# Decoder layer on one core: the merge and output stages with a recorded load queue, five gate buffers, w_o's second half split later, and another last norm

## Chip, cores, metric

One core of a Trainium2 chip runs the whole program in one launch. The metric is the device time of one execution in microseconds. Engines are named as in the profile: PE is TensorE, PEld its weight loads, DVE is VectorE, ACT is ScalarE, POOL is GpSimd, SP is SyncE, which here only issues transfers.

## What is computed

One decoder layer over 1024 tokens of width 1024, batch 1, all in float32. Only the end of it is touched here:

```
merged = sigmoid(g_conv) * y_conv + sigmoid(g_att) * y_att     # y_att = (att * silu(z_att)) @ w_att_out
x = x + gate * (merged @ w_o)
out = rmsnorm(x) * final_g                                     # x * rsqrt(mean(x*x) + 1e-6) * final_g
```

What comes before it (norm, in-projection, convolution branch, dilated window attention in three groups) is left as it is.

## The kernel before, in words

Products in float32 are made of three products of rounded parts: each operand is split into a high part `hi` (rounded to the type float32r by a copy on ACT, line 57) and a low part `lo` (the difference, on DVE, line 58; the helper is `split`, lines 55 to 58). `mm3` (lines 72 to 75) issues hi·hi, hi·lo and lo·hi into one bank of PSUM.

The merge (lines 1197 to 1224) makes eight tiles `d` of 128 output channels by 1024 tokens, kept transposed (channels in partitions). For tile d, `project` runs two halves of 512 tokens; each half has four steps k, twelve matmuls, over the attention output `ah`, `al` with the weights `w_ao[d]` (256 KB), which were loaded to a buffer `wraw` and split into `whi` and `wlo`. The function `merge` (lines 1219 to 1222) takes the bank: DVE multiplies it by the sigmoid of the attention gate (`sgr`, 512 KB, loaded from the scratch tensor `ascr`; sigmoid on ACT, line 1205), DVE adds the convolution part (`ttr`, 512 KB, from `cscr`), and the sum is split into `hh[d]` and `hl[d]`, the left operand of the output product. The 16 `ascr` half tiles were written by the stage before, through small buffers `gs` (lines 791, 792), the last of them just as the merge begins.

`w_o` has two halves n (512 output columns each) of four parts kp of 512 KB. `w_out` loads and splits one part into `woh[n, kp]`, `wol[n, kp]`. The parts (0,0) to (0,2) are done in the attention stage, (0,3), (1,0) and (1,1) inside the merge at d = 1, 3, 5 (lines 1214 to 1216), and (1,2), (1,3) are recorded behind it (lines 1227 to 1229).

The output (lines 1236 to 1278) makes eight tiles `t` of 128 tokens by 1024 columns. `out_cols` runs 24 matmuls per 512 columns over `hh`, `hl` and w_o, then DVE multiplies by the gate row `gate_b`, adds the residual `xt`, and ACT squares the result and sums it over the columns. `out_norm` makes the inverse root of the mean by a square root on ACT, a reciprocal and one Newton step on DVE (`inv_sqrt`, lines 106 to 114), scales `y` by it and by `final_g` in two halves (line 1266) and writes each half (line 1267). The order is (0,0), (1,0), (0,1), (1,1) by tile and column half, then tiles 2 to 7 whole; tile 7's second half is cut in two pieces of 256 columns, so that it has three sums.

Buffers: `wraw` has three buffers, `whi` and `wlo` two each. The pool `fin` of the last two stages lies over memory of the attention stage's pool, buffer by buffer (a tile waits only for those old tiles that it lies over). Its ring `tmp` holds `sgr`, `ttr`, `xt` and `y` in four buffers of 4 KB per partition.

What sets the order: the attention stage runs in the recorded order on PE, DVE, ACT and SP (`manual_schedule`, line 1133). Behind it, in the merge and the output, a planner sets the order of each engine's instructions and of SP's queue by priorities and its own model of times; each queue is in order at run time, so a waiting instruction holds all that stand behind it.

Of the kernel before, what the change touches and what calls it, by code (L numbers as in the profile page):

```python
# [39 lines left out]
def layer(ctx: ExitStack, tc: tile.TileContext, a, out):  # L40
    nc = tc.nc
    ctx.enter_context(nc.allow_non_contiguous_dma(reason="small gathers of row maxima"))
    add, mult, sub, mx = ALU.add, ALU.mult, ALU.subtract, ALU.max
# [3 lines left out]
    wpool = ctx.enter_context(tc.tile_pool(name="wpool", bufs=2))  # L47
# [48 lines left out]
    gscr = dram.tile([1, D], F32, name="gscr")  # L96
    bscr = dram.tile([2, 512], F32, name="bscr")
    cscr = dram.tile([KT, P, S], F32, name="cscr")
    ascr = dram.tile([KT, P, S], F32, name="ascr")
# [6 lines left out]
    def inv_sqrt(cols, n, tmp):  # L106

        s, y, z = tmp[:, 0:n], tmp[:, n:2 * n], tmp[:, 2 * n:3 * n]
        nc.scalar.activation(s, cols, AF.Sqrt)
        nc.vector.reciprocal(y, s)  # L110
        nc.vector.tensor_mul(z, y, y)
        nc.vector.tensor_mul(z, z, cols)
        nc.vector.tensor_scalar(z, z, -0.5, 1.5, op0=mult, op1=add)
        nc.vector.tensor_mul(cols, y, z)

# [3 lines left out]
    def bank():  # L119
        return pd.tile([P, 512], F32, name="d", tag="d")  # L120
# [50 lines left out]
    with sbuf_pool("start") as st, tc.manual_schedule(  # L171
            engines={nc.tensor.engine, nc.vector.engine, nc.scalar.engine, nc.sync.engine}):
# [192 lines left out]
        for t in range(7):  # L365
# [4 lines left out]
            if t == 3:  # L370
                last = bank()
# [10 lines left out]
        for kt in range(KT):  # L382
# [424 lines left out]
    raws, made_w = {}, {}  # L807
# [34 lines left out]
    k2, q2, v2 = {}, {}, {}  # L842
# [227 lines left out]
    ATT = (("k0", "k1"), ("k2", "q0"), ("q1", "q2"), ("l0", "l1"))  # L1070
    woh, wol = {}, {}

    def w_out(n, kp, pool=None):


        raw = load_raw(a["w_o"][n, kp])
        if not pool and (n, kp) < (0, 3):
            yield
        if pool:
            hi, lo = (pool.tile([P, 1024], F32R, name=f"{x}{n}{kp}") for x in ("oh", "ol"))  # L1080
        elif n == 0 and kp > 1:
            both = parts_tile("oh")
            hi, lo = both[:, 0], both[:, 1]
        else:
            hi, lo = (head_tile(x, "oh") for x in {(0, 0): ("l2", "v0"), (0, 1): ("v1", "v2"), (1, 3): ("k0", "k1")}[n, kp])
        (split if pool or (n, kp) >= (0, 3) else split_late)(hi, lo, raw)
        woh[n, kp], wol[n, kp] = hi, lo
        yield

# [43 lines left out]
    with tc.manual_schedule(engines={nc.tensor.engine, nc.vector.engine, nc.scalar.engine, nc.sync.engine}):  # L1133
        for slot_ in range(-LEAD, 4 * units - LEAD):
# [6 lines left out]
            if VAL <= slot_ < stages + VAL:  # L1141
                n, st_ = divmod(slot_ - VAL, 8)
# [4 lines left out]
            if TURN <= slot_ < stages + TURN:  # L1147
                n, st_ = divmod(slot_ - TURN, 8)
# [3 lines left out]
            if 0 <= slot_ < stages:  # L1152
                n, st_ = divmod(slot_, 8)
# [39 lines left out]
    ahead = ahead_ao[0]  # L1193
# [3 lines left out]
    pd = ctx.enter_context(psum_pool("pd3", bufs=8))  # L1197
    fp = ctx.enter_context(sbuf_pool("fin"))
    def temp4(name):
        return fp.tile([P, S], F32, name=name, tag="tmp", bufs=4)  # L1200

    def gates_load(d):
        sg_, tt = temp4("sgr"), temp4("ttr")
        nc.sync.dma_start(sg_, ascr[d])
        nc.scalar.activation(sg_, sg_, AF.Sigmoid)
        nc.sync.dma_start(tt, cscr[d])
        return sg_, tt

    ahead = ahead, gates_load(0)
    for d in range(KT):  # L1210
        w, (sg_, tt) = ahead
        if d + 1 < KT:
            ahead = weights(a["w_ao"][d + 1], 512), gates_load(d + 1)
        if d in (1, 3, 5):
            for _ in w_out(*((0, 3), (1, 0), (1, 1))[d // 2], fp if d > 1 else None):
                pass
        hi, lo = hh[:, d, :], hl[:, d, :]

        def merge(half, s, ps):
            nc.vector.tensor_mul(sg_[:, s], ps, sg_[:, s])  # L1220
            nc.vector.tensor_add(tt[:, s], tt[:, s], sg_[:, s])
            split(hi[:, s], lo[:, s], tt[:, s])

        project(w, merge, 4, lambda k, s: ah[k][:, s], lambda k, s: al[k][:, s])


    for kp, pool in ((2, fp), (3, None)):
        for _ in w_out(1, kp, pool):
            pass
    gate_b = fp.tile([P, D], F32, name="gate_b")  # L1230
    nc.sync.dma_start(gate_b, gscr.to_broadcast([P, D]))
    fg_b = fp.tile([P, D], F32, name="fg_b")
    nc.sync.dma_start(fg_b, a["final_g"].to_broadcast([P, D]))
    rows, ys, sums_ = {}, {}, {}

    def out_cols(t, n, c0, c1):

        if t not in ys:
            rows[t], ys[t] = temp4("xt"), temp4("y")
            nc.sync.dma_start(rows[t], a["x"][t * P:(t + 1) * P, :])  # L1240
            sums_[t] = fp.tile([P, 3], F32, name="ss", tag="ss", bufs=3)
        xt, y, s = rows[t], ys[t], slice(c0, c1)
        ps = bank()[:, 0:c1 - c0]
        for k in range(KT):
            c = slice(t * P, (t + 1) * P)
            o = (k % 2) * 512 + c0 % 512
            rh, rl = (w[c0 // 512, k // 2][:, o:o + c1 - c0] for w in (woh, wol))
            nc.tensor.matmul(ps, hh[:, k, c], rh, start=k == 0, stop=False)  # L1248
            nc.tensor.matmul(ps, hh[:, k, c], rl, start=False, stop=False)  # L1249
            nc.tensor.matmul(ps, hl[:, k, c], rh, start=False, stop=k == KT - 1)  # L1250
        nc.vector.tensor_mul(y[:, s], ps, gate_b[:, s])
        nc.vector.tensor_add(y[:, s], y[:, s], xt[:, s])
        nc.scalar.activation(xt[:, s], y[:, s], AF.Square, accum_out=sums_[t][:, n:n + 1])

    def out_norm(t):
        y, ss = ys.pop(t), sums_[t]
        r = fp.tile([P, 1], F32, name="r", tag="r", bufs=2)
        tmp = fp.tile([P, 3], F32, name="tmp3", tag="tmp3", bufs=2)
        nc.vector.tensor_add(r, ss[:, 0:1], ss[:, 1:2])
        if t == 7:  # L1260
            nc.vector.tensor_add(r, r, ss[:, 2:3])
        nc.vector.tensor_scalar(r, r, 1.0 / D, EPS, op0=mult, op1=add)
        inv_sqrt(r, 1, tmp)
        for n in range(2):
            s = slice(n * 512, n * 512 + 512)
            nc.vector.scalar_tensor_tensor(y[:, s], y[:, s], r, fg_b[:, s], op0=mult, op1=mult)
            nc.sync.dma_start(out[t * P:(t + 1) * P, s], y[:, s])


    for t, n in ((0, 0), (1, 0), (0, 1), (1, 1)):  # L1270
# [74 lines left out]
```

## Time and profile before

| | |
|---|---|
| median of 3 runs | 1245.23 us (1245.12 to 1245.72) |
| the profiled execution | 1247.03 us |
| its span, first to last instruction | 1245.2 us |
| mean granted TensorE clock | 0.999 of full |
| merge, first to last matmul start | 1104.53 to 1149.75 us |
| output, first to last matmul start | 1149.98 to 1237.21 us |

Times in the profile are counted from the start of the span. Busy time is the time that an engine worked on an instruction; matmuls overlap, so that a matmul lasts 0.39 us but the next begins 0.23 us after it. A row of a timeline gives the start, the duration, engine, line and operation, the tiles written and read, and in brackets how long the engine had been idle and what ended that.

### The profile page before, as it was taken

To read this page: it belongs to the slowest core of one execution; us is meant where nothing else is said; L and a number is where in the kernel's file an instruction comes from. 1 tells how busy PE (TensorE), PEld (TensorE's weight loads), DVE (VectorE), ACT (ScalarE), POOL (GpSimd) and SP (SyncE) were. 2 spreads that over 40 slices of the span, in tenths; PEclk is the share of its full clock that TensorE was granted. 3 is DMA by queue.
4 is the path that set the end of the run, shared out by engine and by line. 5 is a ranking of instruction groups with operands and counts; after the bars stand their busy time and mean duration, and the time that the engine had idled before them with its cause. 6 is when DMAs were issued, how large, how long until landed. Compare 5 with 4: busy or idle time off the path is not lost.

```text
span 1245.2 us, 17007 instructions
## 1 busy us (share of the span) xinstructions
PE 1232.5 (99%) x6234; PEld 1030.9 (83%) x6234; DVE 909.7 (73%) x1500; ACT 512.2 (41%) x1026; POOL 91.0 (7%) x79
## 2 busy tenths in 40 slices
PE   9999999999999999999999999999999999999997
PEld 7787888888888888888888888888888888887886
DVE  7867999999999986873325657777776762458554
ACT  5653112101222235931015666666666664345211
POOL 0000000000000000000031111111111112100000
PEclk9999999999999999999999999999999999999999
DMA  9632311311221112445645555665665564668231
GB/s 359 195 103 74 111 52 51 109 59 51 85 61 43 50 59 76 133 172 194 192 83 153 136 137 142 164 181 145 159 188 142 144 176 131 214 227 291 88 102 68
DMA packets 89896, 165.09 MB, mean 133 GB/s; under 512 B 28563, under 2 KB 42195, under 8 KB 89814
## 3 DMA queue, kind: packets, MB, share of 16 engines
q1 hardware_dynamic: 73136, 157.40, 42.3%
q10 hardware_dynamic: 16678, 6.61, 1.9%
q8 instruction: 49, 0.80, 0.3%
q14 instruction: 33, 0.27, 0.1%
HBM read 105.48 MB, written 27.04 MB: 106 GB/s over the span
## 4 chain that ended last, share of the span: by engine, by line
PE 95%; DVE 2%; DMA 2%; ACT 1%; issue 0%; DVEq 0%; ACTq 0%; SPq 0%
PE d L73 24%; PE d L75 23%; PE d L74 23%; PE o L957 4%; PE s L920 3%; PE t L936 3%; PE d L1249 2%; PE d L1248 2%; PE d L506 2%; PE d L1250 2%; PE d L507 2%; PE d L505 2%; DMA x<-in_xT 1%; PE d L271 1%; DVE wa L166 0%; DVE hl L238 0%
## 5 line engine op out<-in xcount | busy, mean ns | idle before, releaser
L73 PE MATMUL d<-hh,whi 128*128 128x512 f32 x1072 | 421.1, 393 | 0.0
L75 PE MATMUL d<-hh,wlo 128*128 128x512 f32 x1072 | 418.3, 390 | 0.0
L74 PE MATMUL d<-hl,whi 128*128 128x512 f32 x1072 | 417.8, 390 | 0.0
L446 DVE SCALAR_TENSOR_TENSOR v<-u,cw,v 128x1024 f32<-128x1024 f32 x232 | 280.4, 1277 | 0.0
L75 PEld LDWEIGHTS d<-hh,wlo 128*128 128x128 f32 x1072 | 201.2, 188 | 43.1
L73 PEld LDWEIGHTS d<-hh,whi 128*128 128x128 f32 x1072 | 201.4, 188 | 39.2 <-issue 0.2
L74 PEld LDWEIGHTS d<-hl,whi 128*128 128x128 f32 x1072 | 201.5, 188 | 38.7 <-issue 0.2
L57 ACT ACTIVATE whi<-wraw 128x512 fp32r<-128x512 f32 (+1 forms) x104 | 83.9, 827 | 214.6 <-PE d L74 204.6
L58 POOL TENSOR_TENSOR wlo<-wraw,whi 128x512 fp32r<-128x512 f32 (+1 forms) x56 | 81.6, 1475 | 639.7 <-ACT whi L57 639.7
L925 DVE CUSTOM_DVE_ANT_0 sb<-s,mask 128x128 f32<-128x128 f32 (+1 forms) x192 | 59.6, 347 | 59.9 <-PE s L920 59.8
L929 ACT ACTIVATE sb<-sb,stats 128x128 f32<-128x128 f32 (+1 forms) x192 | 84.9, 443 | 32.9 <-DVE stats L925 32.8
L936 PE MATMUL t<-ident,sb 128*128 128x128 f32 x280 | 73.1, 274 | 0.0
L957 PE MATMUL o<-ph,vt 128*64 128x128 f32 (+1 forms) x432 | 68.2, 247 | 0.0
L58 DVE TENSOR_TENSOR wlo<-wraw,whi 128x1024 fp32r<-128x1024 f32 (+1 forms) x48 | 54.8, 1142 | 15.9 <-ACT whi L57 15.3
L751 ACT ACTIVATE ph<-t 128x384 fp32r<-128x384 f32 (+2 forms) x96 | 45.7, 476 | 41.3 <-PE t L936 29.6
L920 PE MATMUL s<-k,q 128*128 128x128 f32 (+1 forms) x192 | 56.9, 302 | 0.0
L754 DVE TENSOR_TENSOR pl<-t,ph 128x384 fp32r<-128x384 f32 (+2 forms) x96 | 51.9, 540 | 6.1 <-ACT ph L751 6.0
L920 PE MATMUL s<-k,ql 128*128 128x128 f32 (+1 forms) x192 | 52.8, 285 | 0.0
L957 PE MATMUL o<-pl,vt 128*64 128x128 f32 (+1 forms) x216 | 52.6, 258 | 0.0
L1248 PE MATMUL d<-oh,hh 128*128 128x512 f32 (+1 forms) x136 | 51.2, 377 | 0.0
L1250 PE MATMUL d<-oh,hl 128*128 128x512 f32 (+1 forms) x136 | 51.2, 377 | 0.0
L672 DVE TENSOR_TENSOR gs<-d,sgc 128x512 f32<-128x512 f32 x16 | 11.1, 691 | 54.9 <-PE d L75 49.3
(242 smaller groups left out, 1914.2 us busy)
## 6 DMA issues: line engine op xcount, KB each, us to landing
wraw<-in_w_t SPq DMA_DIRECT2D x67, 512.0 KB, 4.1
k<-kqp SPq DMA_DIRECT2D x96, 128.0 KB, 2.3
q<-kqp SPq DMA_DIRECT2D x96, 128.0 KB, 2.4
wa<-in_w_ada SPq DMA_DIRECT2D x16, 512.0 KB, 6.7
ql<-kqp SPq DMA_DIRECT2D x48, 128.0 KB, 2.4
wg<-wscr SPq DMA_DIRECT2D x48, 128.0 KB, 3.1
wraw<-in_w_v SPq DMA_DIRECT2D x11, 512.0 KB, 3.6
vscr<-gs SPq DMA_DIRECT2D x16, 256.0 KB, 2.0
```

Of the source, the lines that this page charges most:

```text
L57: nc.scalar.activation(hi, raw, AF.Copy)
L58: (lo_eng or nc.vector).tensor_sub(lo, raw, hi.bitcast(F32))
L73: nc.tensor.matmul(ps, lh, rh, start=start, stop=False)
L74: nc.tensor.matmul(ps, lh, rl, start=False, stop=False)
L75: nc.tensor.matmul(ps, ll, rh, start=False, stop=stop)
L446: nc.vector.scalar_tensor_tensor(d, u[:, k:k + S], cw[:, ct, k:k + 1], d, op0=mult, op1=add)
L920: products.append((w, lambda c=c, w=w, l=x[:, ts_], r=k[:, ks], i=i: nc.tensor.matmul(ps[:, c:c + w], l, r, start=i == 0, stop=i == 1)))
L929: nc.scalar.activation(sb[:, c:c + w], sb[:, c:c + w], AF.Exp, bias=stats[:, t, h, 1:2], scale=-1.0, accum_out=stats[:, t, h, 0:1])
L936: yield from ((lambda c=c: nc.tensor.transpose(ps[:, c:c + P], sb[:, c:c + P], ident)) for c in range(0, o, P))
L957: nc.tensor.matmul(out_, l, r, **kw))
L1248: nc.tensor.matmul(ps, hh[:, k, c], rh, start=k == 0, stop=False)
L1250: nc.tensor.matmul(ps, hl[:, k, c], rh, start=False, stop=k == KT - 1)
```

## The change

- SP's queue runs in the recorded order from the merge to the end (`manual_schedule` for SP); PE, DVE and ACT stay with the planner.
- The ring `tmp` has five buffers. Gates are loaded two tiles ahead (`gate(d + 2)`), the convolution part one tile ahead, `w_ao` two tiles ahead, each at a recorded place.
- Part (0,3) of w_o stays in the merge (d = 1). The four parts of the second half are loaded at d = 5, 6, 7 and after the merge, and split after it. `gate_b` is loaded at d = 6; `fg_b` moves into a `wraw` buffer.
- `xt` is loaded a tile ahead.
- The last norm: the sum of squares, the mean and EPS are spread over other instructions (EPS as a bias of the square root), and Newton's step has three instructions for one column. For tile 7, `y` is multiplied by `final_g` before the norm is known, and the scaling is split: 640 columns on DVE, written by SP, 384 on ACT, written from ACT's queue.

```diff
+    def newton(cols, y, z):
+        if cols.shape[1] == 1:
+            nc.vector.scalar_tensor_tensor(z, y, cols, y, op0=mult, op1=mult)
+        else:
+            nc.vector.tensor_mul(z, y, y)
+            nc.vector.tensor_mul(z, z, cols)
         nc.vector.tensor_scalar(z, z, -0.5, 1.5, op0=mult, op1=add)
         nc.vector.tensor_mul(cols, y, z)
...
+    def w_out_second(kp, raw):
+        if kp < 3:
+            hi, lo = (fp.tile([P, 1024], F32R, name=f"{x}1{kp}") for x in ("oh", "ol"))
+        else:
+            hi, lo = (head_tile(x, "oh") for x in ("k0", "k1"))
+        split(hi, lo, raw)
+        woh[1, kp], wol[1, kp] = hi, lo
...
     def temp4(name):
-        return fp.tile([P, S], F32, name=name, tag="tmp", bufs=4)
-
-    def gates_load(d):
-        sg_, tt = temp4("sgr"), temp4("ttr")
-        nc.sync.dma_start(sg_, ascr[d])
-        nc.scalar.activation(sg_, sg_, AF.Sigmoid)
-        nc.sync.dma_start(tt, cscr[d])
-        return sg_, tt
-
-    ahead = ahead, gates_load(0)
+        return fp.tile([P, S], F32, name=name, tag="tmp", bufs=5)
+
+    def load4(name, src):
+        tile_ = temp4(name)
+        nc.sync.dma_start(tile_, src)
+        return tile_
+
+    ctx.enter_context(tc.manual_schedule(engines={nc.sync.engine}))
+    sgs, tts, raws = {}, {}, {}
+
+    def gate(d):
+        sgs[d] = load4("sgr", ascr[d])
+        nc.scalar.activation(sgs[d], sgs[d], AF.Sigmoid)
+
+    gate(0)
+    tts[0] = load4("ttr", cscr[0])
+    raws[1] = load_raw(a["w_ao"][1], 512)
+    gate(1)
     for d in range(KT):
-        w, (sg_, tt) = ahead
         if d + 1 < KT:
-            ahead = weights(a["w_ao"][d + 1], 512), gates_load(d + 1)
-        if d in (1, 3, 5):
-            for _ in w_out(*((0, 3), (1, 0), (1, 1))[d // 2], fp if d > 1 else None):
+            tts[d + 1] = load4("ttr", cscr[d + 1])
+        if d + 2 < KT:
+            raws[d + 2] = load_raw(a["w_ao"][d + 2], 512)
+            gate(d + 2)
+        w, sg_, tt = ahead, sgs.pop(d), tts.pop(d)
+        if d + 1 < KT:
+            ahead = [wpool.tile([P, 512], F32R, name=x, tag=x) for x in ("whi", "wlo")]
+            split(*ahead, raws.pop(d + 1))
+        if d == 1:
+            for _ in w_out(0, 3):
                 pass
+        if d == 6:
+            gate_b = fp.tile([P, D], F32, name="gate_b")
+            nc.sync.dma_start(gate_b, gscr.to_broadcast([P, D]))
+        if d >= 5:
+            raws[d] = load_raw(a["w_o"][1, d - 5])
...
+    rows = {t: load4("xt", a["x"][t * P:(t + 1) * P, :]) for t in range(2)}
+    raws[8] = load_raw(a["w_o"][1, 3])
+    for kp in range(4):
+        w_out_second(kp, raws.pop(5 + kp))
+    fg_b = wpool.tile([P, D], F32, name="wraw", tag="wraw", bufs=3)
     nc.sync.dma_start(fg_b, a["final_g"].to_broadcast([P, D]))
...
         if t not in ys:
-            rows[t], ys[t] = temp4("xt"), temp4("y")
-            nc.sync.dma_start(rows[t], a["x"][t * P:(t + 1) * P, :])
+            if t > 0 and t < 7:
+                rows[t + 1] = load4("xt", a["x"][(t + 1) * P:(t + 2) * P, :])
+            ys[t] = temp4("y")
...
         nc.scalar.activation(xt[:, s], y[:, s], AF.Square, accum_out=sums_[t][:, n:n + 1])
+        if t == 7:
+            if not n:
+                last.append(temp4("yg"))
+            if n == 2:
+                nc.vector.tensor_scalar(sums_[t][:, 0:1], sums_[t][:, 0:1], sums_[t][:, 1:2], None, op0=add)
+            nc.vector.tensor_mul(last[0][:, s], y[:, s], fg_b[:, s])
...
-        nc.vector.tensor_add(r, ss[:, 0:1], ss[:, 1:2])
-        if t == 7:
-            nc.vector.tensor_add(r, r, ss[:, 2:3])
-        nc.vector.tensor_scalar(r, r, 1.0 / D, EPS, op0=mult, op1=add)
-        inv_sqrt(r, 1, tmp)
-        for n in range(2):
-            s = slice(n * 512, n * 512 + 512)
-            nc.vector.scalar_tensor_tensor(y[:, s], y[:, s], r, fg_b[:, s], op0=mult, op1=mult)
-            nc.sync.dma_start(out[t * P:(t + 1) * P, s], y[:, s])
+        nc.vector.tensor_scalar(r, ss[:, 2:3] if t == 7 else ss[:, 1:2], ss[:, 0:1], 1.0 / D, op0=add, op1=mult)
+        nc.scalar.activation(tmp[:, 0:1], r, AF.Sqrt, bias=eps)
+        nc.vector.tensor_scalar(r, r, EPS, None, op0=add)
+        nc.vector.reciprocal(tmp[:, 1:2], tmp[:, 0:1])
+        newton(r, tmp[:, 1:2], tmp[:, 2:3])
...
+        else:
+            y = last[0]
+            nc.scalar.activation(y[:, 640:1024], y[:, 640:1024], AF.Copy, scale=r)
+            nc.vector.tensor_scalar(y[:, 0:640], y[:, 0:640], r, None, op0=mult)
+            nc.scalar.dma_start(out[t * P:(t + 1) * P, 640:1024], y[:, 640:1024])
+            nc.sync.dma_start(out[t * P:(t + 1) * P, 0:640], y[:, 0:640])
```

## Rows read from the trace of the kernel before

**Rows 1.** The page: busy time and share of each engine, and the granted TensorE clock in 40 equal slices of the span, in tenths of full speed.
```profile
PE 1232.5 (99%) x6234; PEld 1030.9 (83%) x6234; DVE 909.7 (73%) x1500; ACT 512.2 (41%) x1026; POOL 91.0 (7%) x79
...
PEclk9999999999999999999999999999999999999999
```

**Rows 2.** Busy time by stretch, the merge and the output: stretch, its length, busy time of PE, PEld, DVE, ACT and POOL with the number of instructions, then the granted clock, the busy share of the DMA engines and GB/s.
```profile
1104.50:1150.10 45.60, 44.05 (x194) 36.00 (x193) 33.86 (x52) 24.41 (x33) 0.00 (x0) 1.00 0.86 289
1150.10:1237.50 87.40, 87.39 (x409) 73.15 (x407) 44.76 (x104) 17.23 (x45) 0.00 (x0) 1.00 0.27 90
```

**Rows 3.** The longest wait of PE in the whole span: who waited for whom, us in total, times, the longest.
```profile
PE d L75 <- DVE wlo L58: 1.6, 1, 1.6
```

**Rows 4.** Timeline of PE: the first matmul of merge tiles 0 and 1, three around the hole in tile 6, and the first matmul of the output.
```profile
1104.53 0.39 PE L73 MATMUL d<-ah,whi 128*128 128x512 f32 x1
...
1109.96 0.39 PE L73 MATMUL d<-ah,whi 128*128 128x512 f32 x1
...
1137.44 0.39 PE L74 MATMUL d<-ah,whi 128*128 128x512 f32 x1
1139.38 0.50 PE L75 MATMUL d<-ah,wlo 128*128 128x512 f32 x1 [1.55 <-DVE wlo L58]
1139.72 0.40 PE L73 MATMUL d<-ah,whi 128*128 128x512 f32 x1
...
1149.98 0.39 PE L1248 MATMUL d<-oh,hh 128*128 128x512 f32 x1
```

**Rows 5.** Timeline of DVE ahead of the hole.
```profile
1136.29 1.23 DVE L58 TENSOR_TENSOR ol<-wraw,oh 128x1024 fp32r<-128x1024 f32 x1
...
1138.64 0.69 DVE L58 TENSOR_TENSOR wlo<-wraw,whi 128x512 fp32r<-128x512 f32 x1
```

**Rows 6.** Timeline of SP's queue around the start of the merge; equal instructions that follow one another are one row.
```profile
1091.97 5.55 SPq L62 DMA_DIRECT2D wraw<-in_w_ao  x3
...
1105.31 0.95 SPq L62 DMA_DIRECT2D wraw<-in_w_ao  x2
1106.31 0.45 SPq L1204 DMA_DIRECT2D sgr<-ascr  x1
1108.98 0.33 SPq L1206 DMA_DIRECT2D ttr<-cscr  x1
1109.36 0.42 SPq L1204 DMA_DIRECT2D sgr<-ascr  x1
1109.83 0.43 SPq L1206 DMA_DIRECT2D ttr<-cscr  x1
```

**Rows 7.** Waits of SP's queue from 1050 us to the end, one row of them.
```profile
SPq L1206 <- DMA ascr<-gs: 2.1, 1, 2.1
```

**Rows 8.** Timeline of ACT at the start of the merge: the write of the last gate half.
```profile
1105.70 0.33 ACTq L792 DMA_DIRECT2D ascr<-gs  x1
```

**Rows 9.** Transfers: issuing queue, count, size, median us from issue to landing; the first two from 1093 to 1096.9 us, the third from 1100 us to the end; and the time to landing of the eight `ttr` loads.
```profile
ascr<-gs ACTq DMA_DIRECT2D x1, 256.0 KB, 2.2
wraw<-in_w_ao SPq DMA_DIRECT2D x1, 256.0 KB, 2.7
...
xt<-in_x SPq DMA_DIRECT2D x8, 512.0 KB, 3.8
...
DMA to landing us min/median/max: 4.0/5.7/7.5
```

**Rows 10.** Groups of instructions from 1100 us to the end, shapes apart: total and mean ns of one | idle before.
```profile
L58 DVE TENSOR_TENSOR wlo<-wraw,whi 128x512 fp32r<-128x512 f32 x7 | 4.8, 686 | 4.7 <-ACT whi L57 4.7
L57 ACT ACTIVATE whi<-wraw 128x512 fp32r<-128x512 f32 x7 | 4.3, 621 | 4.8 <-PE d L74 4.8
L58 DVE TENSOR_TENSOR ol<-wraw,oh 128x1024 fp32r<-128x1024 f32 x3 | 3.7, 1221 | 0.0
```

**Rows 11.** Timeline of the tail, all engines: the last matmul, the last square and its sum, the first and the last step of the norm, the scaling (two instructions).
```profile
1237.21 0.28 PE L1250 MATMUL d<-oh,hl 128*128 128x256 f32 x1
...
1238.44 0.42 ACT L1253 ACTIVATE xt<-y 128x256 f32<-128x256 f32 x1 [2.37 <-DVE y L1252]
...
1238.98 0.16 DVE L1261 TENSOR_TENSOR r<-r,ss 128x1 f32<-128x1 f32 x1 [0.57 <-ACT xt L1253]
...
1240.43 0.16 DVE L114 TENSOR_TENSOR r<-tmp 128x1 f32<-128x1 f32 x1
1240.63 1.41 DVE L1266 SCALAR_TENSOR_TENSOR y<-y,r,fg_b 128x512 f32<-128x512 f32 x2
```

**Rows 12.** Transfers from 1240 to 1246 us: what they moved, in 40 slices of 0.15 us, and the two last writes with their time to landing.
```profile
GB/s 0 0 0 0 0 0 0 0 0 0 0 0 0 0 55 300 396 410 369 355 382 410 396 369 55 0 0 0 0 0 0 0 0 0 0 0 0 0 0 0
...
out<-y SPq DMA_DIRECT2D x2, 256.0 KB, 2.1
```

**Rows 13.** Groups of instructions in the whole span: a tensor-scalar on DVE with two scalar operands and with one, and the square on 512 columns on ACT.
```profile
L440 DVE TENSOR_SCALAR v<-u,cw,cvec 128x1024 f32<-128x1024 f32 x8 | 6.4, 806 | 0.0
...
L442 DVE TENSOR_SCALAR v<-u,cw 128x1024 f32<-128x1024 f32 x8 | 6.0, 746 | 0.0
...
L1253 ACT ACTIVATE xt<-y 128x512 f32<-128x512 f32 x15 | 9.5, 633 | 61.4 <-DVE y L1252 61.4
```

**Rows 14.** Busy time by stretch behind the last matmul, columns as in rows 2.
```profile
1241.00:1242.00 1.00, 0.00 (x0) 0.00 (x0) 1.00 (x2) 0.00 (x0) 0.00 (x0) 1.00 0.00 0
1242.00:1243.00 1.00, 0.00 (x0) 0.00 (x0) 0.04 (x1) 0.00 (x0) 0.00 (x0) 0.54 0.76 283
```

More of the change, by code (lines that the diff above doesn't have):

```diff
@@ L110, in inv_sqrt @@
         nc.vector.reciprocal(y, s)
-        nc.vector.tensor_mul(z, y, y)
-        nc.vector.tensor_mul(z, z, cols)
+        newton(cols, y, z)
+    def newton(cols, y, z):
[4 more added lines that the diff above has]
+            nc.vector.tensor_mul(z, z, cols)
         nc.vector.tensor_scalar(z, z, -0.5, 1.5, op0=mult, op1=add)
@@ L1071, in layer, with w_out @@
     woh, wol = {}, {}
-    def w_out(n, kp, pool=None):
+    def w_out_second(kp, raw):
[5 more added lines that the diff above has]
+        woh[1, kp], wol[1, kp] = hi, lo
+    def w_out(n, kp):
         raw = load_raw(a["w_o"][n, kp])
-        if not pool and (n, kp) < (0, 3):
+        if kp < 3:
             yield
-        if pool:
-            hi, lo = (pool.tile([P, 1024], F32R, name=f"{x}{n}{kp}") for x in ("oh", "ol"))
-        elif n == 0 and kp > 1:
+        if kp > 1:
             both = parts_tile("oh")
@@ L1084, in w_out @@
         else:
-            hi, lo = (head_tile(x, "oh") for x in {(0, 0): ("l2", "v0"), (0, 1): ("v1", "v2"), (1, 3): ("k0", "k1")}[n, kp])
-        (split if pool or (n, kp) >= (0, 3) else split_late)(hi, lo, raw)
+            hi, lo = (head_tile(x, "oh") for x in (("l2", "v0"), ("v1", "v2"))[kp])
+        (split if kp == 3 else split_late)(hi, lo, raw)
         woh[n, kp], wol[n, kp] = hi, lo
@@ L1224, in layer @@
         project(w, merge, 4, lambda k, s: ah[k][:, s], lambda k, s: al[k][:, s])
[L1227 to L1232, printed above, removed]
+    rows = {t: load4("xt", a["x"][t * P:(t + 1) * P, :]) for t in range(2)}
[3 more added lines that the diff above has]
+    fg_b = wpool.tile([P, D], F32, name="wraw", tag="wraw", bufs=3)
     nc.sync.dma_start(fg_b, a["final_g"].to_broadcast([P, D]))
-    rows, ys, sums_ = {}, {}, {}
+    ys, sums_ = {}, {}
     def out_cols(t, n, c0, c1):
         if t not in ys:
-            rows[t], ys[t] = temp4("xt"), temp4("y")
-            nc.sync.dma_start(rows[t], a["x"][t * P:(t + 1) * P, :])
+            if t > 0 and t < 7:
+                rows[t + 1] = load4("xt", a["x"][(t + 1) * P:(t + 2) * P, :])
+            ys[t] = temp4("y")
             sums_[t] = fp.tile([P, 3], F32, name="ss", tag="ss", bufs=3)
@@ L1253, in out_cols @@
         nc.scalar.activation(xt[:, s], y[:, s], AF.Square, accum_out=sums_[t][:, n:n + 1])
+        if t == 7:
[4 more added lines that the diff above has]
+            nc.vector.tensor_mul(last[0][:, s], y[:, s], fg_b[:, s])
+    last = []
+    eps = fp.tile([P, 1], F32, name="eps")
+    nc.gpsimd.memset(eps, EPS)
     def out_norm(t):
@@ L1258, in out_norm @@
         tmp = fp.tile([P, 3], F32, name="tmp3", tag="tmp3", bufs=2)
-        nc.vector.tensor_add(r, ss[:, 0:1], ss[:, 1:2])
-        if t == 7:
-            nc.vector.tensor_add(r, r, ss[:, 2:3])
-        nc.vector.tensor_scalar(r, r, 1.0 / D, EPS, op0=mult, op1=add)
-        inv_sqrt(r, 1, tmp)
-        for n in range(2):
-            s = slice(n * 512, n * 512 + 512)
-            nc.vector.scalar_tensor_tensor(y[:, s], y[:, s], r, fg_b[:, s], op0=mult, op1=mult)
-            nc.sync.dma_start(out[t * P:(t + 1) * P, s], y[:, s])
+        nc.vector.tensor_scalar(r, ss[:, 2:3] if t == 7 else ss[:, 1:2], ss[:, 0:1], 1.0 / D, op0=add, op1=mult)
[3 more added lines that the diff above has]
+        newton(r, tmp[:, 1:2], tmp[:, 2:3])
+        lo, hi = slice(0, 512), slice(512, 1024)
+        if t < 7:
+            for s in (lo, hi):
+                nc.vector.scalar_tensor_tensor(y[:, s], y[:, s], r, fg_b[:, s], op0=mult, op1=mult)
+                nc.sync.dma_start(out[t * P:(t + 1) * P, s], y[:, s])
+        else:
[4 more added lines that the diff above has]
+            nc.sync.dma_start(out[t * P:(t + 1) * P, 0:640], y[:, 0:640])
     for t, n in ((0, 0), (1, 0), (0, 1), (1, 1)):
```

## The prediction

> **What bounds the kernel now.** I read the page first: TensorE is busy for 1232.5 of 1245.2 us, at the full granted clock (2.4 GHz) in every slice [rows 1]. So nothing that runs beside TensorE is worth anything; only its idle time and what lies behind its last matmul can be won. The windows over the two stages that the change touches say the same by stage: 44.05 us busy of 45.60 in the merge, 87.39 of 87.40 in the output [rows 2]. The waits of TensorE name the one hole: 1.6 us, once, for `wlo` [rows 3]. Its timeline places it: in merge tile 6 the third product waits until 1139.38 [rows 4]. The reader should see that eight merge tiles take 1149.98 − 1104.53 = 45.45 us, and at the pitch of tile 0 (1109.96 − 1104.53 = 5.43) would take 43.44. The merge holds 2.0 us of loss, not 1.6, since the first matmuls after the hole are slow too (0.34 us instead of 0.23 to the next). The reason is VectorE's order: `wlo` of tile 6 came behind an `ol` split of w_o (1.23 us) and other merge work [rows 5]. Behind the last matmul (start 1237.21) lie 8 us: multiply, add, square, a chain of eight short steps, two scalings, two writes [rows 11, 12].
>
> 0.2% of this kernel is 2.49 us, about what a measurement can tell from no change: below 1242.74 is faster, above 1247.72 slower. The most that the merge (2.0) and a modest tail can give is close to that line, so any loss decides.
>
> **The merge, the gain.** The three w_o splits that the merge now issues for the second half (1.22 us of VectorE each [rows 10]) move behind it, and `w_ao` and the gates are asked for two tiles ahead. Then `wlo` of tile d+1 has its data one tile sooner, and no `ol` stands in front of it. The moved splits fall into the first 10.9 us of the output stage (tiles (0,0) and (1,0), which use the first half only), where VectorE is half idle (44.76 of 87.40 [rows 2]); four of them need 4.9 us. Their cover is that order of the output tiles; without it they would cost up to 4.9. The fourth one's load waits for the first one's split, and is wanted last, some 15 us into the stage. Gain: 2.0 us; bounds 0 (another late split takes its place) and 2.0 (TensorE cannot go under its pitch).
>
> **The merge, the new wait.** SP's queue is now in recorded order: sgr 0, ttr 0, w_ao 1, sgr 1, ttr 1, w_ao 2, and so on. Before, the w_ao loads of tiles 1 and 2 had been taken ahead (three w_ao loads from 1091.97, two more at 1105.31), and ttr 0 left at 1108.98 only, behind a wait of 2.1 us for the last gate write `ascr<-gs` [rows 6, 7]. That wait is about memory: the pool of the merge lies over buffers of the attention stage, its first tile takes the first buffer of the ring and the second tile the last, and the last lay over `gs`. With five buffers the last one begins 4 KB further on; by the addresses of the compiled kernel before it would run from byte 194,240 to 198,336 of a partition, and the second `gs` from 193,728 to 195,776. So ttr 0 still waits for that write, and now w_ao 1 is queued behind it, and all of sgr 1, ttr 1, w_ao 2 after it. Who waits for w_ao 1: ScalarE's `whi`, VectorE's `wlo`, and TensorE, which wants them at 1109.96 [rows 4].
>
> Worked out: the last `gs` write is issued at 1105.70 [rows 8]; with nothing else on the queues (SP stands still) I take its landing as the 2.2 us of an earlier one [rows 9], so ttr 0 leaves at 1107.9 and w_ao 1 at 1108.3 (0.33 per issue [rows 6]). Landing of w_ao 1: alone 2.7 us, 1111.0; strictly behind ttr 0, which as a 512 KB load takes 3.8 (the row of `xt`), plus the 1.1 by which 512 KB takes longer than 256 KB: 1112.8 [rows 9]. I take 1111.8, as both transfers overlap. `whi` takes 0.62: 1112.4; first matmul 1112.5; `wlo` (0.69) is ready at 1113.15 where the third product would start at 1112.95, with the slow restart 0.3 to 0.4 more [rows 10, 4]. **Stall: 2.9 us.** Lower bound 2.0 (landing alone); upper 5.6: the write lands as late as before (+1.1), w_ao 1 strictly behind (+1.0), and one `hh` of tile 0 ahead of `whi` on ScalarE (+0.6).
>
> After that the queue has slack: ttr d+1 is asked for when the sum of tile d−1 is done and is wanted two tiles (10.9 us) later, against 4.0 to 7.5 us to landing [rows 9]; w_ao d+2 follows it and is wanted a tile and a half later. Each tile moves 1.28 MB in 5.43 us, 240 GB/s, where the merge before ran at 289 [rows 2]. I cost the rest at nothing; the cover is that slack, and if the merge lagged by a tile a `wlo` stall like the old one (up to 2.0) would be back. gate_b, x and final_g are asked for later than before, but several us ahead of use.
>
> **The tail.** The steps after the last square: before add, scale, sqrt, reciprocal, four Newton steps, 1238.98 to 1240.63. After: one step with a tensor scalar (dearer: a tensor-scalar with one such operand takes 746 ns on 1024 columns, with two 806, so 0.06 each [rows 13]), sqrt, then the EPS add, which overwrites what sqrt reads and so follows it, reciprocal, three Newton steps, one with a tensor scalar. One step fewer of about 0.19 (0.20 between starts [rows 11]), minus 0.12 for two dearer operands: −0.1. The extra multiply by final_g (256 columns, 0.42) fits beside the square (0.52 to its sum). The scaling: instead of two steps of 0.7 one after the other, 640 columns on VectorE (0.746 × 640/1024, about 0.5) beside 384 on ScalarE (between 0.42 for 256 and 0.63 for 512 columns [rows 11, 13]: 0.52, starting 0.1 later). Both end at about 1241.1, where before the first half's write left at 1241.4 and the second's at 1242.1. The bytes then set the end: before, 0.52 MB moved without a pause from 1242.1 to 1243.6 at 350 to 410 GB/s [rows 12], so the second write hardly waited for its scaling. After, the same bytes start when the first write leaves, 0.3 sooner. **Gain 0.3**; bounds 0 (two queues start worse) and 0.95 (each write lands 2.1 us after its own issue, bytes no limit).
> The Trainium skill, DMA: Bandwidth & Descriptors, section "Issuing engines are not separate DMA queues", says that transfers started by different engines run on the same 16 DMA engines and interleave, and that a second issuer saves only issue time. By that rule the write on ScalarE's queue is worth at most one issue, and the tail gives 0.3; by two independent queues it would give 0.95, and the total below would be 1245.2.
>
> **Sum.** −2.0 + 2.9 − 0.3 = +0.6 us. The profiled execution took 1247.03 us (span 1245.2), 1.8 more than the median of the runs; against it the changed kernel would take 1247.6, and against the median of 1245.23, **1245.8**.
>
> **Rivals.**
> (B) The first wait is not there: the fifth buffer lies clear of `gs`, or the queue is not held as I think, and w_ao 1 lands before 1109. For it: the first tile of that pool waited for nothing, and sgr 1 and ttr 1 left 0.4 to 0.5 us apart with no wait of their own [rows 6]. Against it: ttr 0 did wait, for a buffer that moves by only 4 KB [rows 7]. Then −2.0 − 0.3 = −2.3: 1242.9, between 1242.3 (tail at its upper bound) and 1243.5.
> (C) Slower: the same stall at tile 1, but long. `gs` lands as late as before, so ttr 0 leaves at 1108.98 and w_ao 1 at 1109.35, lands strictly behind it at 1113.9, and `whi` stands behind `hh` of tile 0: TensorE restarts near 1115.2, stall 5.2, sum +2.9: 1248.1. It decides from a stall of 4.8. A granted clock that falls would add to it: after the last matmul the clock stayed at its full level until 1242.0, some 4.5 us, and was half (1.2 GHz) from then [rows 14], so 2.9 us should leave it alone and 5.2 may not; a tile at half clock would add up to 5.4. Against it: the quiet queues.
> (D) The edits of the merge do nothing that TensorE sees: the old hole goes and a like one comes elsewhere, only the tail is left: 1244.9. It lies inside the main case.
>
> **How the numbers follow.** Main case with (D): 0.68, own range 1244.3 to 1247.7. (B): 0.20, of which somewhat under half below 1242.74. (C): 0.12. The range 1242.7 to 1247.8 leaves out the lower part of (B) and most of (C). Faster by over 0.2%: 0.12 (from (B), and a little for a tail better than its bound); slower 0.12; within 0.2%: 0.76.
>
> **What would show it.** Right: TensorE's waits have one of 2 to 4 us at the start of merge tile 1 for `whi` or `wlo`, and none at tile 6; on SP ttr 0 leaves at about 1108 with a wait for `ascr<-gs`, sgr 0 near 1092, w_ao 1 right behind ttr 0; the tail from the last matmul's start to the end of the span is 7.7 instead of 8.0 us. Wrong: w_ao 1 leaves SP before 1106 (B), or the stall is over 4.8 or the granted clock in the merge is below 1 (C), or TensorE waits in the output stage for the second half of w_o, which I cost at nothing.

## The result, and the profile after

The changed kernel takes 1248.95 us (median of 20 runs, 1247.51 to 1249.85) against 1245.85 for the kernel before beside it; the ratio is 1.002 [1.0014, 1.0026]. I had forecast 1245.8 and a range up to 1247.8: the change costs 1.7 to 3.2 us by that interval (3.1 between the two medians), and the result lies 1.15 us above the range. The changed kernel's times stand in two groups: 8 runs at 1247.5 to 1248.2 and 12 at 1248.9 to 1249.9. The profiled execution took 1249.25.

Busy time of the merge and of the output in the kernel after, columns as in [rows 2]:

```profile
1105.90:1152.60 46.70, 44.26 (x195) 36.00 (x194) 34.44 (x53) 24.86 (x34) 0.00 (x0) 1.00 0.78 270
1152.50:1239.90 87.40, 87.40 (x409) 73.28 (x408) 46.01 (x99) 18.66 (x45) 0.00 (x0) 1.00 0.30 103
```

The output is full, as before. The merge still has a hole. TensorE's waits in the kernel after:

```profile
PE d L73 <- ACT whi L57: 2.4, 1, 2.4
...
PE t L942 <- DVE pl L760: 1.3, 1, 1.3
```

Timeline of TensorE: the first matmul of the merge, the last seen of tile 0, the first two of tile 1, the first of the output, the last of all:

```profile
1106.00 0.39 PE L73 MATMUL d<-ah,whi 128*128 128x512 f32 x1
...
1111.21 0.39 PE L75 MATMUL d<-ah,wlo 128*128 128x512 f32 x1
1113.97 0.50 PE L73 MATMUL d<-ah,whi 128*128 128x512 f32 x1 [2.37 <-ACT whi L57]
1114.31 0.39 PE L74 MATMUL d<-ah,whi 128*128 128x512 f32 x1
...
1152.55 0.39 PE L1281 MATMUL d<-oh,hh 128*128 128x512 f32 x1
...
1239.78 0.28 PE L1283 MATMUL d<-oh,hl 128*128 128x256 f32 x1
```

The old hole of tile 6 is gone [rows 3, 4]; a longer one stands at the start of tile 1. The merge takes 1152.55 − 1106.00 = 46.55 us, 1.10 more than before. It also starts 1.47 us later than in [rows 4], although the change does not touch what comes before it. SP's queue names the cause of the new hole (against [rows 6, 7]): the load of `ttr` is held from 1093 to 1108.98, with `w_ao` 1 behind it. Its timeline, then the row of its waits:

```profile
1092.23 0.33 SPq L62 DMA_DIRECT2D wraw<-in_w_ao  x1
1092.61 0.53 SPq L1217 DMA_DIRECT2D sgr<-ascr  x1
1108.98 0.33 SPq L1217 DMA_DIRECT2D ttr<-cscr  x1
1109.40 0.38 SPq L62 DMA_DIRECT2D wraw<-in_w_ao  x1
```
```profile
SPq L1217 <- DMA ascr<-gs: 15.6, 1, 15.6
```

ScalarE's timeline has both ends of it: the last gate write, and `whi` of tile 1, which waited for that `w_ao`:

```profile
1106.83 0.33 ACTq L798 DMA_DIRECT2D ascr<-gs  x1
...
1113.29 0.63 ACT L57 ACTIVATE whi<-wraw 128x512 fp32r<-128x512 f32 x1 [3.75 <-DMA wraw<-in_w_ao]
```

The tail, all engines: last square, first and last step of the norm, the scaling, the writes (against [rows 11]); then the transfers from 1240 to 1247.4 us in 40 slices, with the times to landing (against [rows 12]):

```profile
1241.01 0.42 ACT L1286 ACTIVATE xt<-y 128x256 f32<-128x256 f32 x1 [2.37 <-DVE y L1285]
...
1241.55 0.21 DVE L1302 TENSOR_SCALAR r<-ss 128x1 f32<-128x1 f32 x1
...
1242.83 0.16 DVE L120 TENSOR_TENSOR r<-tmp 128x1 f32<-128x1 f32 x1
1243.02 0.61 ACT L1314 ACTIVATE yg<-yg,r 128x384 f32<-128x384 f32 x1 [0.93 <-DVE r L120]
1243.02 0.55 DVE L1315 TENSOR_SCALAR yg<-yg,r 128x640 f32<-128x640 f32 x1
1243.60 0.33 SPq L1317 DMA_DIRECT2D out<-yg  x1
1243.67 0.34 ACTq L1316 DMA_DIRECT2D out<-yg  x1
```
```profile
GB/s 0 0 0 0 0 0 0 0 0 0 0 0 0 0 0 0 0 0 0 0 0 0 0 28 360 401 401 379 376 349 349 191 0 0 0 0 0 0 0 0
...
out<-yg SPq DMA_DIRECT2D x1, 320.0 KB, 2.4
out<-yg ACTq DMA_DIRECT2D x1, 192.0 KB, 2.6
```

From the start of the last matmul to the end of the span it is 7.65 us, before 8.03.

**One sum for all executions.** In every trace of this study the output stage takes 87.23 or 87.24 us from its first to its last matmul. What differs is where the merge starts, how long it takes, and the tail: 1245.15 us with the old tail or 1244.8 with the new one, plus (start − 1104.6) plus (merge − 43.5), gives each execution's time to 0.05 us (the six experiments below too). It is bookkeeping: it tells where the time lies, not why.

| execution | merge starts | merge takes | time |
|---|---|---|---|
| before, profiled | 1104.53 | 45.45 | 1247.03 |
| before_again | 1104.60 | 44.56 | 1246.22 |
| before_look_a | 1104.70 | 44.12 | 1245.87 |
| before_look_b | 1104.64 | 43.57 | 1245.30 |
| after, profiled | 1106.00 | 46.55 | 1249.25 |
| after_again | 1105.06 | 47.73 | 1249.47 |
| after_look_a | 1104.95 | 46.29 | 1247.93 |
| after_look_b | 1104.41 | 47.69 | 1248.78 |

The floor of the merge is what eight full tiles without a wait take, 43.5 us [rows 4]. So three things are to be explained: the merge of before, which lies 0.1 to 2.0 us over its floor; the merge of after, which lies 2.8 to 3.1 or 4.2 us over it; and the late start.

### The profile page after: what moved, and what is told of

It reads as the page before. It is cut to its first block, busy times and chain, and to the rows that moved or that the text cites. A ratio compares the mean times of both kernels' runs of the same rounds, so it can differ in the third digit from the quotient of the medians.

```text
span 1247.4 us, 16999 instructions
## 1 busy us (share of the span) xinstructions
PE 1232.9 (99%) x6234; PEld 1030.9 (83%) x6234; DVE 911.8 (73%) x1494; ACT 514.1 (41%) x1027; POOL 91.1 (7%) x80
## 4 chain that ended last, share of the span: by engine, by line
PE 91%; DVE 3%; DMA 3%; ACT 2%; issue 1%; SPq 0%; DVEq 0%; ACTq 0%
PE d L73 22%; PE d L75 22%; PE d L74 22%; PE o L963 4%; PE s L926 3%; PE d L1281 2%; PE d L1283 2%; PE d L513 2%; PE d L511 2%; PE d L1282 2%; PE d L512 2%; PE t L942 2%; DMA x<-in_xT 1%; PE d L277 1%; DMA sgr<-ascr 1%
```

## The experiments

**The two kernels again.** Both kernels unchanged, beside the experiments.

> The kernel before, unchanged, for a second trace of it. Theory 1 (the change alone, in merge and tail, makes the difference): the same span as the first trace, 1245.2 us, with no hole of TensorE in the attention stage. Theory 2 (part of the difference is an accident of that stage: a VectorE split of the values, `vt`, that meets a weight split on GpSimd lasts 2.4 to 2.6 us instead of 0.43, and TensorE then loses about 1.5 us): the spans of single executions stand in steps of about 1.5 us, and a trace that is 1.5 shorter than the first one lacks the long `vt` at 995.7 us.

> The changed kernel, unchanged, for a second trace. Both theories: TensorE waits 2.4 us for `whi` at merge tile 1 in every execution, and merge and tail together cost 0.7 us more than before (merge 46.55 instead of 45.45 us, tail 7.6 instead of 8.0). Theory 2: an execution without the long `vt` at 1009.8 us is 1.5 us shorter (span 1245.8), one with it 1247.2 to 1247.4.

Measured: before 1246.22 us, 1.0001 [0.9992, 1.0009] of the kernel before; after 1249.13, 1.0021 [1.0012, 1.0031]. The wait at tile 1 is there again (2.3 us). Theory 2 does not hold for the meeting at 995.7 us: the trace of before_again lacks the long `vt` there, before_look_a and before_look_b have it (2.44 us), and all three start the merge at 1104.6 to 1104.7. after_again has no long `vt` at 1009.8 us, but it took 1249.47 us and was not 1.5 us shorter, since its merge took 47.73 us; why is asked below.

**The load order at the start of the merge, and the ring's place.** In e1 the weights of tiles 1 and 2 are asked for ahead of the gates:

```diff
+    for d in (1, 2):
+        raws[d] = load_raw(a["w_ao"][d], 512)
     gate(0)
     tts[0] = load4("ttr", cscr[0])
-    raws[1] = load_raw(a["w_ao"][1], 512)
     gate(1)
...
-            raws[d + 2] = load_raw(a["w_ao"][d + 2], 512)
+            if d:
+                raws[d + 2] = load_raw(a["w_ao"][d + 2], 512)
```

> The changed kernel with the loads of w_ao 1 and w_ao 2 recorded ahead of sgr 0 and ttr 0; nothing else is moved. If the hole at tile 1 is the load of w_ao 1 queued behind ttr 0's wait: no wait of TensorE in the merge over 0.3 us, the merge 43.5 to 43.8 us instead of 46.55, and the time 2.8 us below the changed kernel's (ratio to the kernel before 0.9995 to 1.0005 with the attention stage as it fell there, 0.998 if that stage costs nothing). If the hole comes from the order of ScalarE's and VectorE's work at the start of the merge instead: a hole of 2 us or more stays.

In e2 the queue's order stays, and the tile `gate_b` is made first in the pool, so that the ring lies 4 KB further on:

```diff
     fp = ctx.enter_context(sbuf_pool("fin"))
+    gate_b = fp.tile([P, D], F32, name="gate_b")
...
-            gate_b = fp.tile([P, D], F32, name="gate_b")
```

> The changed kernel with the tile gate_b asked for first in the pool of the merge, so that the ring of five buffers begins 4 KB further on and the buffer of ttr 0 no longer lies over the gate buffers `gs`; its load is still issued at tile 6, and the recorded order of the queue is the same. If ttr 0 waits for that memory: ttr 0 and w_ao 1 leave about 5 us earlier, near 1103 to 1105 us (behind the last use of a row buffer of the attention stage), no hole at tile 1, and sgr 1 now waits for `gs`, so that w_ao 2 may come up to 0.7 us late for tile 2; the merge 43.5 to 44.5 us. If ttr 0 waits for anything else: unchanged, a hole of 2.4 us at tile 1.

Measured: e1 1245.29 us, 0.9991 [0.9982, 1.0]; e2 1244.94, 0.9988 [0.9979, 0.9997]; both some 4 us below the changed kernel on the same chip (1249.13). e2 lies below the kernel before beside it, by 0.03 to 0.21%; e1's interval reaches 1. Merge: e1 44.28 (over the 43.8 I had expected at most; a wait of 0.3 us for `wlo` in a later tile is left), e2 43.52, the floor of eight full tiles [rows 4]. e2's SP queue at the merge, and the wait in it:

```profile
1101.83 0.33 SPq L1218 DMA_DIRECT2D ttr<-cscr  x1
1102.20 1.15 SPq L62 DMA_DIRECT2D wraw<-in_w_ao  x1
1107.56 0.32 SPq L1218 DMA_DIRECT2D sgr<-ascr  x1
```
```profile
SPq L1218 <- DMA ascr<-gs: 4.1, 1, 4.1
```

With the same order and other addresses the wait for the gate write has moved from `ttr` 0 to `sgr` 1, behind `w_ao` 1, which leaves 2.4 us ahead of the merge's start instead of 3.4 behind it. So it was a wait about memory and the queue behind it, both at once. `ttr` 0 left earlier than I had expected (1103 to 1105).

**Is it the idle time that halves the clock?** Two more executions of the changed kernel, after_look_a and after_look_b, tell the two groups apart.

> One more execution of the changed kernel. Theory: 1244.9 us (the kernel with the ring moved) plus the merge's excess over 43.5 us plus what the start of the merge is later than 1104.6; with no fall of the clock the excess is about 3 us (1247.6 to 1248.0), with a fall about 4.5 (1249.0 to 1249.5). Rival (the two groups come from something else): a time near 1249 without half clock in the merge and without a late start of it, or one near 1247.6 with it.

> As after_look_a: 1244.9 us plus the merge's excess over 43.5 us plus its late start, within 0.3 us.

Measured 1247.93 and 1248.78, the theory's sums to 0.1 us (1248.0 and 1248.9); both waits are 2.3 us long. after_look_a around the restart, columns as in [rows 2]:

```profile
1111.50:1112.50 1.00, 0.00 (x0) 0.00 (x0) 0.00 (x0) 0.32 (x1) 0.00 (x0) 1.00 1.05 346
1112.50:1113.50 1.00, 0.64 (x3) 0.55 (x4) 0.66 (x2) 0.31 (x1) 0.00 (x0) 1.00 0.92 287
```

after_look_b, the same:

```profile
1111.50:1112.50 1.00, 0.20 (x1) 0.20 (x2) 0.22 (x1) 0.63 (x1) 0.00 (x0) 0.93 0.84 287
1112.50:1113.50 1.00, 1.00 (x3) 0.81 (x4) 1.00 (x3) 0.00 (x0) 0.00 (x0) 0.50 0.99 344
...
1115.50:1116.50 1.00, 1.00 (x5) 0.83 (x4) 0.31 (x1) 1.00 (x3) 0.00 (x0) 0.86 0.96 293
1116.50:1117.50 1.00, 1.00 (x6) 0.83 (x5) 0.49 (x2) 0.70 (x2) 0.00 (x0) 1.00 0.99 360
```

The granted clock (the column behind POOL) is half, 1.2 GHz, from about 1112.4 to 1115.8: the second row holds three matmuls, the last six. The merge takes 47.69 − 46.29 = 1.40 us more. By the mean granted clock of each run (0.997, otherwise 0.998 or more) 18 of 32 runs of the changed kernel had such a fall; of e1, e2 and the kernel before, 2 in 92, so a fall can also come, rarely, without this wait. In the 20 runs of the result 10 fell; the other two of the upper group (1249.25 and 1249.85) did not, and the one with a trace, 1249.25, has the late start in its place.

The fall need not come while TensorE waits. In after_again the matmuls were back at 1112.96 and the clock fell 1.3 us later, at about 1114.3:

```profile
1113.00:1114.00 1.00, 1.00 (x5) 0.83 (x6) 1.00 (x2) 0.00 (x0) 0.00 (x0) 1.00 0.84 295
1114.00:1115.00 1.00, 1.00 (x4) 0.78 (x3) 0.96 (x3) 0.41 (x1) 0.00 (x0) 0.64 0.99 381
```

The end of every trace shows the same spread. TensorE stops there for good, and the clock falls some time after the end of its last matmul: 4.6, 2.7, 2.3 and 4.7 us in the four executions of before, and from 1.9 (e4, an experiment below) to 5.0 us (e2) over all 14 traces. e4's last matmul, and the window in which its clock falls (at about 1238.2):

```profile
1235.98 0.28 PE L1250 MATMUL d<-oh,hl 128*128 128x256 f32 x1
...
1238.00:1239.00 1.00, 0.00 (x0) 0.00 (x0) 0.58 (x4) 0.20 (x1) 0.00 (x0) 0.59 0.00 0
```

e3 computes the second half of tile 0 twice (`fill` is 4 there and 0 elsewhere), so that TensorE works through the wait:

```diff
             ps = bank()
+            for k in range(fill * half):
+                c = slice(k * P, (k + 1) * P)
+                mm3(ps, hi[:, c], lo[:, c], rh(k, s), rl(k, s), k == 0, k == fill - 1)
             for k in range(n_k):
```

> The changed kernel, but the second half of merge tile 0 is computed twice: twelve matmuls more (2.7 us at the tile's pitch of 5.43 us for 24), so that TensorE works on in the time in which it waited for w_ao 1. The transfers and their order stay. Theory (the granted clock falls in part of the runs because TensorE stood idle for 2.4 us): the wait at tile 1 is under 0.5 us, the first matmuls of tile 1 run at the usual 0.23 us pitch, no run shows half clock behind it, and the times stand in one group at 1247.3 to 1247.7 instead of two (1247.6 and 1249.1); merge about 46.3 us. Rival (the clock falls for a reason that has nothing to do with the idle stretch): half of the runs still lie 1.5 us above the others. Second rival (the wait is not for data but TensorE's own): the wait stays behind the twelve matmuls and the kernel takes 2.7 us more, 1250.3 or above.

Measured: 1247.96 us, 1.0015 [1.0006, 1.0025]; nine of eleven runs at 1247.6 to 1248.1, one with a mean clock of 0.997 (1251.29, no trace), and the profiled one at 1250.20, whose merge starts 2.4 late. Its first matmul of the merge and of the output:

```profile
1107.01 0.39 PE L73 MATMUL d<-ah,whi 128*128 128x512 f32 x1
...
1153.48 0.39 PE L1284 MATMUL d<-oh,hh 128*128 128x512 f32 x1
```

46.47 us with twelve matmuls more (12 × 0.227 = 2.7), and TensorE names no wait in it. The extra work costs nothing beside the kernel without a fall, and the upper group is gone. That it lies 0.3 above what I expected is within the spread of the lower group. The unchanged kernel did not run on e3's chip; on the chip of after_again 7 of its 10 runs fell.

e5 makes the wait longer, by asking for `w_ao` 1 behind `sgr` 1:

```diff
-    raws[1] = load_raw(a["w_ao"][1], 512)
     gate(1)
+    raws[1] = load_raw(a["w_ao"][1], 512)
```

> The changed kernel, with the load of w_ao 1 asked for behind that of the second gate tile (sgr 1), 512 KB more ahead of it: the wait at merge tile 1 grows from 2.4 to about 3.5 to 4.5 us (0.4 for the issue, 1.1 to 1.5 for the bytes, up to 0.9 if the sigmoid of that tile goes ahead of whi). Theory (an idle stretch brings the fall of the clock, the surer the longer it is): nearly all runs show the fall, a few us at 1.2 GHz behind the wait, 1.5 us more, and stand in one group, 1250.2 to 1251.2. Rival (the fall comes by chance, whatever the length of the wait): two groups again, 1.5 us apart, at about 1248.9 and 1250.4 in equal parts.

Measured: 1251.97 us (1251.11 to 1252.10, five runs), 1.0044 [1.0032, 1.0057], each with a mean clock of 0.996 or 0.997. TensorE's longest wait, then windows from the wait to the end of the half clock:

```profile
PE d L73 <- ACT whi L57: 4.1, 1, 4.1
```
```profile
1111.50:1112.50 1.00, 0.00 (x0) 0.00 (x0) 0.74 (x2) 0.31 (x1) 0.00 (x0) 1.00 0.96 277
1112.50:1113.50 1.00, 0.00 (x0) 0.00 (x0) 0.00 (x0) 0.75 (x1) 0.00 (x0) 0.73 0.93 350
...
1119.50:1120.50 1.00, 1.00 (x5) 0.78 (x5) 0.62 (x1) 0.00 (x0) 0.00 (x0) 0.85 0.93 356
```

With 4.1 us of idle time all runs fall, as the theory has it; the time lies 0.8 us above what I had expected at most, since the clock is already half when work comes back and stays so for some 5.4 us. With the wait filled 1 run in 11 falls, with 2.3 to 2.4 us of it 18 in 32, with 4.1 us 5 in 5. So the idle time brings the fall; what decides in a single execution with the shorter wait is not shown.

**What was the old hole worth?** Two more executions of before, and the kernel before with one part of w_o moved behind the merge:

> One more execution of the kernel before. Theory (its executions differ by the length of the hole in merge tile 6): time less the merge's excess over 43.5 us is the same in each: 1247.03 - 1.95 = 1245.1 and 1246.22 - 1.06 = 1245.2 so far, so this one takes 1245.1 to 1245.3 plus its own excess, within 0.3. Rival (the executions differ elsewhere): no such sum.

> As before_look_a: 1245.1 to 1245.3 us plus the merge's excess over 43.5 us, within 0.3 us; an instruction of VectorE held by GpSimd near 1010 us would add up to 2.4 us upstream of the merge and show as a later start of the merge than 1104.6.

Measured: 1245.87 us with a merge of 44.12, 1245.30 with one of 43.57; less the excess over 43.5 that is 1245.25 and 1245.23. Both are as expected. In before_look_b there is no hole at all:

```profile
1104.64 0.39 PE L73 MATMUL d<-ah,whi 128*128 128x512 f32 x1
...
1148.21 0.39 PE L1248 MATMUL d<-oh,hh 128*128 128x512 f32 x1
```

The four executions of before run VectorE's work at tile 6 in the same order: twice `sgr`, then the `ol` split, twice `ttr`, then `wlo`. So the split ahead of `wlo` alone makes no hole. What differs is when this row of work can begin, behind the sigmoid of the gate, which waits 2.21, 1.71, 0.80 and 0.66 us for the gate's load where the hole is 1.55, 0.74, 0.29 and 0 us. ScalarE in the profiled execution, then in before_look_b:

```profile
1133.99 1.06 ACT L1205 ACTIVATE sgr<-sgr 128x1024 f32<-128x1024 f32 x1 [2.21 <-DMA sgr<-ascr]
```
```profile
1132.23 1.06 ACT L1205 ACTIVATE sgr<-sgr 128x1024 f32<-128x1024 f32 x1 [0.66 <-DMA sgr<-ascr]
```

No run moves that load by itself, so its part is argued from these four traces. e4 takes the split away:

```diff
-        if d in (1, 3, 5):
+        if d in (1, 3):
...
-    for kp, pool in ((2, fp), (3, None)):
+    for kp, pool in ((1, fp), (2, fp), (3, None)):
```

> The kernel before, with one edit: part (1,1) of w_o is loaded and split behind the merge with (1,2) and (1,3), not at merge tile 5. It prices the old hole of merge tile 6 by itself, with the old queue and the old tail. My prediction took 2.0 us for it, from one execution; another execution of the same kernel showed a merge of 44.56 us, 1.0 over what eight full tiles take. Theory 1 (the typical hole is 1.0 us or less, the profiled one was a long one): merge 43.5 to 44.0 us in the trace and a time 0.5 to 1.0 us below the kernel before. Theory 2 (2.0 us as predicted): 2.0 us below. Rival (another late split takes its place, since the planner orders DVE anew): merge 44.5 or more and no gain.

Measured: 1246.18 us, 1.0001 [0.9993, 1.001]: no gain. Its merge takes 44.15; tile 6 is clean, and a smaller hole stands in tile 7:

```profile
1143.61 0.50 PE L75 MATMUL d<-ah,wlo 128*128 128x512 f32 x1 [0.33 <-DVE wlo L58]
```

That is nearest the rival, another late split, though its merge is shorter than the 44.5 foreseen there; this edit alone does not price the hole. Four executions of before do.

**The late start.** In the profiled execution of after, VectorE and GpSimd met at 1009.8 us, in the attention stage. First that kernel, then the kernel before at the same place:

```profile
1009.73 2.39 POOL L58 TENSOR_TENSOR wlo<-wraw,whi 128x1024 fp32r<-128x1024 f32 x1 [11.90 <-ACT whi L57]
...
1009.78 2.62 DVE L760 TENSOR_TENSOR vt<-vr,vt 128x256 fp32r<-128x256 f32 x1
```
```profile
1009.77 0.42 DVE L754 TENSOR_TENSOR vt<-vr,vt 128x256 fp32r<-128x256 f32 x1
...
1010.19 2.42 POOL L58 TENSOR_TENSOR wlo<-wraw,whi 128x1024 fp32r<-128x1024 f32 x1 [12.35 <-ACT whi L57]
```

The same VectorE instruction takes 2.62 us instead of 0.42 when GpSimd's split has begun 0.05 us ahead of it; the softmax behind it is late (TensorE waits 1.3 us for `pl`, the row shown above), and all later work by 1.4. e3's execution has the same meeting (2.61 us, a late start of 2.4), the other three traces of after do not. The like meeting at 995.7 us, in all of these traces of after, delays nothing that can be seen in the start of the merge. e6 is e2 with these eight splits on VectorE:

```diff
-            split(hi, lo, raws.pop(u), nc.gpsimd)
+            split(hi, lo, raws.pop(u))
```

> The changed kernel with the moved ring (no wait at merge tile 1), and the eight low parts of the gate weights (128x1024, 2.4 us each on GpSimd) made on VectorE, 1.22 us each. Theory (a VectorE instruction that begins while GpSimd splits lasts until that ends, 2.4 instead of 0.43 us, and such a meeting at 1009.8 us put 1.5 us into the profiled execution of the changed kernel): no vt or wg instruction over 2 us behind 990 us, the merge begins at 1104.3 to 1104.6 in the trace, the times lie at 1244.5 to 1244.9 and no run is 1.5 us above the others. Rival (the eight splits hold VectorE's queue in its recorded order, the softmax behind them is late): 0.5 to 1 us more at each of several places, 1247 or above.

Measured: 1246.23 us (1245.88 to 1246.79), 1.0001 [0.9992, 1.001]. No VectorE instruction over 2 us is left behind 990 us, but the merge starts at 1105.86: at 1009.76 VectorE first waits 0.5 us for ScalarE's `whi` and then splits for 1.22, ahead of the softmax. Both theories were half right, and neither had the time: the meetings are gone, and the split in VectorE's own queue makes the merge 1.3 us late in the trace; all eleven runs lie 0.9 us or more above e2's median. So e6 does not price the meeting, and that it delays the merge by 1.4 us rests on the two traces that have it.

## Why the prediction was wrong

- **The new wait: right.** With the merge 1.47 later, `ttr` 0 left at 1108.98 (1107.9 foreseen, 1109.4 with the shift), 2.15 us behind the gate write (2.2), `w_ao` 1 0.42 behind it, and `whi` began 3.9 behind that (3.5). The merge lies 46.55 − 43.52 (e2) = 3.0 us over its floor; I had 2.9. e2 shows the lapped buffer, e1 the queue.
- **The tail: right.** 0.38 us (0.3). By the Trainium skill, DMA: Bandwidth & Descriptors, "Issuing engines are not separate DMA queues", two issuers share the same 16 DMA engines; the trace agrees: bytes from both queues moved at 349 to 401 GB/s, no faster than from one [rows 12].
- **The split of w_o's second half and loads at nothing: right.** No wait in the output stage, merge at its floor in e2.
- **The step from the profiled execution to the median: wrong, 2.0 us.** I took 2.0 us for the old hole from one execution and then set the sum against a median 1.8 us lower. But that 1.8 was the hole: an execution at 1245.3 has none (its merge is 0.07 over the floor). The same 2 us were taken away twice. Against the profiled execution the forecast was 1247.6, where the lower group stands; without a hole in the median, 1245.23 + 2.9 − 0.38 is 1247.8. My own lower bound for the gain, 0, with the stall of 2.9 gives this too; the range of the main case did not put the two together. And 1245.23 was the median of three short executions: the 20 runs beside the change have 1245.85, those beside the experiments 1246.62 and 1246.11.
- **The reason of the old hole: half right.** I put it down to VectorE's order. That order is the same in the execution without a hole; in the four traces the hole grows with the wait for the gate's load in front of it, which no run moves by itself.
- **The clock at nothing: wrong, 1.4 us in about half of the runs.** I read from [rows 14] that 2.9 us of idle time leave the clock alone, since it stayed full for 4.5 us behind the last matmul. One such row is no bound: in the other executions of before it fell 2.3 to 4.7 us behind the last matmul, and with the wait of 2.3 us it fell in after_look_b and after_again. The median stands in the upper group, and that is partly chance: with 18 falls in 32 runs it could as well have stood near 1247.7, just inside my range, and the forecast of 1245.8 would still have been 2 us off for the reason above. In rival (C) I had put this price behind a stall of 5.2.
- **The late start: not foreseen,** 1.4 us in the profiled execution. It comes from an untouched stage and is not in the other three traces of after (their starts lie within 0.5 us of 1104.6). Whether the change makes it more frequent stays open; no run here tells.

Together: 1245.23 + 2.9 − 0.38 + 1.4 = 1249.15, against 1248.95. So two steps failed, the hole that was subtracted from a median without it, and the price of nothing for the clock behind the new wait; the wait itself was as forecast.

## What to carry to other kernels

Before a stall is subtracted from a median, ask whether the median has it: an execution above the median by just the stall's length says that it has not, and a second trace of the old kernel would have shown it (a hole of 0.7 us in before_again instead of 1.55). A wait of TensorE costs more than its length where the clock may fall behind it, so price a stall with both outcomes. When a ring gets another buffer or a queue its recorded order, list which old tile each new buffer lies over and what stands behind its load; moving the ring was worth 4 us here, and so was the order of two loads.

## What the runs showed of the hardware

- The granted clock fell after 2.3 us of idle time in some executions and not in others of the same program, with the same wait (after_look_b, after_look_a). It could fall when the matmuls were back already (1.3 us into them in after_again). It came back some 3.5 us into the new work in after_look_b, 4.7 in after_again, 5.4 in e5.
- Behind the last matmul of the program it fell after 1.9 to 5.0 us over 14 traces, 2.3 to 4.7 in four executions of the same kernel.
- A VectorE `tensor_sub` of two operands in SBUF that began just after a GpSimd one (0.05 us in the profiled execution of after) lasted until that one had ended (2.62 against 0.42 us). The Trainium skill, SBUF — State Buffer, "Who interferes with whom", states it: the two engines share a read port, an instruction with two operands in SBUF needs it, and one engine holds it at a time. The trace agrees, also in that `pl`, which reads one operand from PSUM, kept its 0.55 us beside GpSimd's split in the kernel before (1011.33 us).
